# State-space layer: the products with the carried state of both channel halves stand together, ahead of the products within the chunks

## The chip, the cores and the metric

The kernel runs on one core of one Trainium2 chip. The metric is the device time of one execution in microseconds (us); less is better. Before the change it is 1345.12 us, the median of three runs (1344.85 to 1346.7).

## What is computed

The kernel is a trunk of two layers, in float32, for one sequence of 512 tokens and 1024 channels. The first layer mixes tokens with a short gated convolution, the second with a state-space mixer (Mamba-2, chunked form); a SwiGLU feed-forward network follows each. The change lies in the state-space mixer, which has 8 groups of 4 heads with 64 channels each. Cut to what matters, the reference is:

```python
def ssd_chunked(xh, dt, a, bm, cm):
    ...
    cb = jnp.einsum('bclgn,bcsgn->bclsg', cm, bm)
    y_diag = jnp.einsum('bclsgr,bcsgrp->bclgrp', cb[..., None] * decay, xdt)
    states = jnp.einsum('bclgn,bclgr,bclgrp->bcgrpn', bm, decay_to_end, xdt)
    ...
    _, prev = lax.scan(step, h0, (jnp.moveaxis(states, 1, 0), jnp.moveaxis(chunk_decay, 1, 0)))
    ...
    y_off = jnp.einsum('bclgn,bcgrpn,bclgr->bclgrp', cm, prev, jnp.exp(cs).astype(dtype))
    return (y_diag + y_off).reshape(bsz, s, g, r, p)
```

`y_off` is the part that the carried state `prev` gives; `y_diag` is the part from within a chunk. Both are added.

## The kernel before

The 512 tokens are cut into 4 chunks of 128 (`NCH = 4`). The 256 channels of a group are two halves `q` of 128, each with two heads of 64. The loop over the groups is a pipeline written out by hand: while group `g` goes through its state-space steps, the projections of group `g+1` (six of them, `ip`, each 24 matmuls of 128x128 by 512 at lines L276 to L278) fill the time of PE. A block `tc.manual_schedule` holds PE, ACT and DVE to the order in which the code issues their instructions; the listings below show what the build made of it.

The steps of a group are, in order: `step_a` (transposes `xtok` L1205 and `btokp` L1216, products `cb` L1222), `states` (products `st` L1238 and L1240, and on DVE the scan that makes `prev`, L1243 and L1245), `step_cc`, and `sums` (the squares of the result are summed over the channels by a product with ones, `ssg`, L1318, in the last group L1315). After `sums`, ACT takes the root (`rg`, L1322), DVE its reciprocal (L1326), and the result is scaled.

`step_cc` is what the change touches. For one half `q`, `step_c` issues on PE:

- 3 products `yo` (L1277), one for each chunk but the first: `prev` (128 x 128) is the stationary operand, so the whole array of 128 rows by 128 columns is used;
- 8 products `yd` (L1283), two heads in each of 4 chunks: a stationary operand of 128 x 64 each, with the output of one head on partitions 0 to 63 and of the other on 64 to 127, so each uses one half of the array's columns.

All of these are float32, and a float32 product shows as two records in the trace: 6 records of `yo`, 16 of `yd`. On DVE, `step_c` then issues four instructions: `y1` = `yo` times the decay (L1288), `y0` = `xs` times `d` plus `yd` (L1289), their sum (L1290), and the gate (L1291). ACT squares the result (L1294, L1297).

PSUM tiles of the tag `aux` (`xtok`, `btokp`, `cb`, `st`, `yo`, `yd`, `ssg`, and in the last group the tiles `y` of the second half of the output projection) go round in 4 buffers, in the order in which they are asked for. In the last group the PE work around `step_cc` is the output projection `y` (L378 to L380), whose weights `whlo` are copied by ACT (L203) and split by DVE (L204).

The weights of a projection come by DMA from SP's queue into `wst`, ACT copies the high part (L221) and DVE makes the low part (L222).

Of the kernel before, what the change touches and what calls it, by code (L numbers as in the profile page):

```python
# [35 lines left out]
def trunk_kernel(  # L36
# [23 lines left out]
    def aux_ps(name, shape=(P, T)):  # L60
        return ps.tile(list(shape), F32, tag="aux", name=name, bufs=4)

    def t2(name):
        return tmp.tile([P, T], F32, tag="t2", name=name, bufs=4)
# [505 lines left out]
    with ExitStack() as ph:  # L570
# [428 lines left out]
        with tc.manual_schedule(engines={PE_ENGINE, mybir.EngineType.SP, mybir.EngineType.Activation,  # L999
# [15 lines left out]
            for k in range(2 * NF - 6):  # L1015
# [8 lines left out]
                q, j = divmod(k - 3, 4)  # L1024
# [25 lines left out]
    with ExitStack() as ph:  # L1050
# [99 lines left out]
        class Group:  # L1150
# [114 lines left out]
                dve.tensor_tensor(e, e, flat(self.cbm).unsqueeze(1).to_broadcast([P, 2, T]), MUL)  # L1265

            def step_cc(self):
                self.step_c(0)
                self.step_c(1)

            def step_c(self, q):

                g = self.g
                pyo = aux_ps("yo")
                for cc in range(1, NCH):
                    sl = slice(cc * P, (cc + 1) * P)
                    pe.matmul(pyo[:, sl], self.prev[:, cc - 1, q * P:(q + 1) * P], self.ct[:, sl],  # L1277
                              start=True, stop=True)
                pyd = aux_ps("yd")
                for cc in range(NCH):  # L1280
                    sl = slice(cc * P, (cc + 1) * P)
                    for hh in range(2):
                        pe.matmul(pyd[hh * HD:(hh + 1) * HD, sl],  # L1283
                                  self.xdt[:, cc, (2 * q + hh) * HD:(2 * q + hh + 1) * HD],
                                  self.e[:, 2 * q + hh, sl], start=True, stop=True)
                y0 = yp.tile([P, T], F32, tag="y", name=f"yg{2 * g + q}")
                y1 = t2("y1")
                dve.tensor_mul(y1[:, P:], pyo[:, P:], self.ecs[:, q, P:])  # L1288
                dve.scalar_tensor_tensor(y0, self.xs[q], dcol[:, 2 * g + q:2 * g + q + 1], pyd, MUL, ADD)  # L1289
                dve.tensor_add(y0[:, P:], y0[:, P:], y1[:, P:])  # L1290
                dve.tensor_mul(y0, y0, self.zs[q])  # L1291
                if q == 0:
                    self.accg = t2("accg")
                    act.activation(self.accg, y0, AF.Square)  # L1294
                else:
                    sqg = t2("sqg")
                    act.activation(sqg, y0, AF.Square)  # L1297
                    if g < NG - 1:
                        pool.tensor_tensor(self.accg, self.accg, sqg, ADD)
                    else:  # L1300
                        dve.tensor_add(self.accg, self.accg, sqg)
                ygs.append(y0)
# [795 lines left out]
```

## Time and profile before

| | |
|---|---|
| time, median of 3 runs | 1345.12 us (1344.85 to 1346.7) |
| the profiled execution: its own time | 1345.17 us |
| the profiled execution: span from first to last instruction | 1343.0 us |
| granted TensorE clock, mean | 0.999 |
| PE busy | 1326.6 us (99%) |
| DVE busy | 985.2 us (73%) |
| ACT busy | 618.2 us (46%) |
| POOL busy | 65.3 us (5%) |

What lies outside the span is 1345.17 - 1343.0 = 2.17 us. In the rows of the trace, PE is the stream of matmuls and PEld that of the weight loads, which may run beside matmuls; DVE, ACT, POOL and SP are the other engines. A row of the timeline gives start, length, engine, line, operation and tiles, and how many records it merges; a bracket gives how long the engine was idle before it and what ended that. A row of the chain of waits gives start, length, and what the time went to. PE's record of a matmul is longer than the distance to the next one, since matmuls are pipelined, so the cost of a matmul on PE is read from the distance of two starts.

### The profile page before, as it was taken

The page shows a single profiled execution, that of the slowest core. Times are in us where ns is not written, and L with a number is a line of the kernel's source. Part 1 is how long each engine was busy: PE and PEld are TensorE (multiplying, and loading weights), DVE is VectorE, ACT ScalarE, POOL GpSimd, SP SyncE. Part 2 cuts the span into 40 slices and gives each one's busy share as a digit, 9 for nine tenths or more (in the row PEclk, how much of TensorE's full clock was granted, in tenths as well). Part 3 has the DMA queues.
Part 4 walks back from the last instruction along what each step waited for, and adds up shares of the span by engine and source line. Part 5 has one row for each costly group of instructions (what it writes and reads, how often), then busy time and mean ns, then how long its engine had stood idle before and what let it go on. Part 6 is the DMA issues. An engine that isn't in the chain of part 4 may idle for free.

```text
span 1343.0 us, 19136 instructions
## 1 busy us (share of the span) xinstructions
PE 1326.6 (99%) x7485; PEld 1143.8 (85%) x7485; DVE 985.2 (73%) x1581; ACT 618.2 (46%) x995; POOL 65.3 (5%) x82
## 2 busy tenths in 40 slices
PE   8999999999999999999999999999999999999997
PEld 7788889888888888898888888888889999998875
DVE  5588866778787322659889988888677777767887
ACT  5323356222323211665644555554474555544664
POOL 0000000000000000000000000000000111101320
PEclk9999999999999999999999999999999999999999
DMA  9757760777776322513543344423251788779851
GB/s 311 237 179 233 252 206 1 225 245 234 238 247 221 126 94 67 157 33 118 165 130 114 91 128 124 132 73 125 79 157 46 192 219 210 199 200 286 166 108 63
DMA packets 199886, 215.90 MB, mean 161 GB/s; under 512 B 8292, under 2 KB 148468, under 8 KB 198772
## 3 DMA queue, kind: packets, MB, share of 16 engines
q1 hardware_dynamic: 186384, 184.74, 44.3%
q0 software_dynamic: 9264, 17.04, 7.4%
q10 hardware_dynamic: 4148, 12.90, 3.0%
q8 instruction: 59, 0.97, 0.3%
q14 instruction: 31, 0.25, 0.1%
HBM read 195.37 MB, written 2.24 MB: 147 GB/s over the span
## 4 chain that ended last, share of the span: by engine, by line
PE 91%; issue 3%; DMA 2%; ACT 2%; DVE 1%; SPq 0%; DVEq 0%; ACTq 0%; POOLq 0%
PE ip L276 14%; PE ip L278 14%; PE ip L277 14%; PE sA L1694 6%; PE y L378 6%; PE y L380 6%; PE y L379 6%; PE cA L1789 4%; PE sC L1694 3%; PE li L756 2%; PE li L276 2%; PE li L277 2%; PE li L278 2%; PE sB L1694 2%; PE yd L1283 1%
## 5 line engine op out<-in xcount | busy, mean ns | idle before, releaser
L276 PE MATMUL ip<-h,whl 128*128 128x512 f32 x840 | 331.2, 394 | 0.2 <-DVE cv L863 0.2
L278 PE MATMUL ip<-h,whl 128*128 128x512 f32 x840 | 327.2, 390 | 0.0
L277 PE MATMUL ip<-h,whl 128*128 128x512 f32 x840 | 327.0, 389 | 0.0
L276 PEld LDWEIGHTS ip<-h,whl 128*128 128x128 f32 x840 | 157.8, 188 | 33.8 <-issue 1.8
L278 PEld LDWEIGHTS ip<-h,whl 128*128 128x128 f32 x840 | 157.7, 188 | 33.4
L277 PEld LDWEIGHTS ip<-h,whl 128*128 128x128 f32 x840 | 157.8, 188 | 31.6
L222 DVE TENSOR_TENSOR whl<-wst,whl 128x1024 fp32r<-128x1024 f32 x99 | 120.4, 1221 | 60.1 <-ACT whl L221 59.9
L124 DVE SCALAR_TENSOR_TENSOR ada_acc<-ada_st,csil,ada_acc 128x512 f32<-128x512 f32 x140 | 105.0, 750 | 3.9 <-DMA ada_st<-in_ada_w_dram 0.4
L204 DVE TENSOR_TENSOR whlo<-wsto,whlo 128x1024 fp32r<-128x1024 f32 x41 | 49.9, 1224 | 78.2 <-ACT whlo L203 78.0
L221 ACT CAST whl<-wst 128x1024 fp32r<-128x1024 f32 x99 | 103.0, 1041 | 3.2 <-DMA wst<-in_a_w_in_dram 1.8
L276 PE MATMUL li<-h,whl 128*128 128x256 f32 x288 | 83.2, 289 | 0.0
L278 PE MATMUL li<-h,whl 128*128 128x256 f32 x288 | 81.6, 283 | 0.0
L277 PE MATMUL li<-h,whl 128*128 128x256 f32 x288 | 81.5, 283 | 0.0
L203 ACT CAST whlo<-wsto 128x1024 fp32r<-128x1024 f32 x41 | 42.6, 1050 | 76.4 <-PE y L380 75.0
L1694 PE MATMUL sA<-tq,whl 128*128 128x256 f32 x576 | 74.6, 283 | 0.3 <-DVE g L1720 0.3
L1694 PEld LDWEIGHTS sA<-tq,whl 128*128 128x128 f32 x576 | 71.6, 192 | 0.6 <-DVE g L1720 0.5
L378 PE MATMUL y<-whlo,ff 128*128 128x512 f32 x176 | 68.6, 390 | 0.0
L380 PE MATMUL y<-whlo,ff 128*128 128x512 f32 x176 | 68.5, 389 | 0.0
L379 PE MATMUL y<-whlo,ff 128*128 128x512 f32 x176 | 68.5, 389 | 0.0
L1142 DVE SCALAR_TENSOR_TENSOR cu<-ip,cols,cu 128x511 f32<-128x511 f32 (+2 forms) x84 | 62.8, 747 | 3.9 <-ACT cu L1139 1.4
L1789 PE MATMUL cA<-whlo,ao 128*128 128x512 f32 x264 | 61.2, 390 | 4.4 <-ACT ao L1767 4.0
L1789 PEld LDWEIGHTS cA<-whlo,ao 128*128 128x128 f32 x264 | 49.3, 188 | 15.7 <-ACT ao L1767 4.8
(328 smaller groups left out, 2436.0 us busy)
## 6 DMA issues: line engine op xcount, KB each, us to landing
ada_st<-in_ada_w_dram SPq DMA_DIRECT2D x96, 512.0 KB, 5.2
wst<-in_f_w_in_dram SPq DMA_DIRECT2D x26, 1024.0 KB, 6.5
wst<-in_m_w_in_dram SPq DMA_DIRECT2D x14, 1024.0 KB, 5.4
wsto<-in_f_w_out_dram SPq DMA_DIRECT2D x10, 1024.0 KB, 5.1
wst<-in_m_w_in_dram SPq DMA_DIRECT2D x20, 512.0 KB, 5.2
wst<-in_a_w_in_dram SPq DMA_DIRECT2D x9, 1024.0 KB, 5.9
wsu<-in_f_w_in_dram SPq DMA_DIRECT2D x17, 512.0 KB, 5.8
csb<-cs_d ACTq DMA_DIRECT2D x8, 1024.0 KB, 5.2
```

The source lines that it names most:

```text
L124: dve.scalar_tensor_tensor(acc, w, csil[:, k:k + 1], acc, MUL, ADD)
L221: later.append((lambda sw=sw, w=w: act.copy(w[:, 0, :nk, :], sw), lambda sw=sw, w=w: dve.tensor_tensor(w[:, 1, :nk, :], sw, w[:, 0, :nk, : ...
L222: lambda sw=sw, w=w: dve.tensor_tensor(w[:, 1, :nk, :], sw, w[:, 0, :nk, :].bitcast(F32), SUB)))
L276: pe.matmul(dst, w_at(w, 0, kk), a[:, 0, sl], start=start, stop=False)
L277: pe.matmul(dst, w_at(w, 0, kk), a[:, 1, sl], start=False, stop=False)
L278: pe.matmul(dst, w_at(w, 1, kk), a[:, 0, sl], start=False, stop=stop)
L378: pe.matmul(pst, a[:, 0, tk], wt[:, 0, kk, :], start=k == 0, stop=False)
L379: pe.matmul(pst, a[:, 0, tk], wt[:, 1, kk, :], start=False, stop=False)
L380: pe.matmul(pst, a[:, 1, tk], wt[:, 0, kk, :], start=False, stop=k == K - 1)
L1142: dve.scalar_tensor_tensor(u[:, sft:], pst[:, :T - sft], w[3 - sft], u[:, sft:], MUL, ADD)
L1694: pe.matmul(dst, w[:, wl, k0 + k, :], moving(q, k, al), skip_group_check=True, start=q in ("P1", "P5", "P2") and k == 0 and i == 0, stop=k ...
L1789: pe.matmul(bank[r][sub], a[:, al, q, tk], w[:, hl, q, :], start=first and k == 0, stop=last and k == 2, skip_group_check=True)
```

## The change

`step_cc` now issues the `yo` products of both halves first and then calls `step_c` for each half, which gets its `yo` tile as an argument. Nothing else is edited; the lines behind move by 5.

```diff
             def step_cc(self):
-                self.step_c(0)
-                self.step_c(1)
-
-            def step_c(self, q):
-
-                g = self.g
+                off = [self.step_o(q) for q in range(2)]
+                for q in range(2):
+                    self.step_c(q, off[q])
+
+            def step_o(self, q):
+
                 pyo = aux_ps("yo")
                 for cc in range(1, NCH):
                     sl = slice(cc * P, (cc + 1) * P)
                     pe.matmul(pyo[:, sl], self.prev[:, cc - 1, q * P:(q + 1) * P], self.ct[:, sl],
                               start=True, stop=True)
+                return pyo
+
+            def step_c(self, q, pyo):
+
+                g = self.g
                 pyd = aux_ps("yd")
                 for cc in range(NCH):
                     sl = slice(cc * P, (cc + 1) * P)
```

PE's instructions in the second group, before (`ip` is the projection around the step; the names in brackets are the semaphores that an instruction waits for, by the engine or DMA queue that raises them):

```order
L278 MATMUL ip<-h_4402,whl 128x512
L1277 MATMUL yo<-ct,prev 128x128 [waits DVE_49,Activation_49]
L1277 MATMUL yo<-ct,prev 128x128 [waits DVE_49] x2
L1283 MATMUL yd<-csb,xdt 64x128 [waits DMAHW6_49,PE_49]
L1283 MATMUL yd<-csb,xdt 64x128 x7
L1277 MATMUL yo<-ct,prev 128x128 x3
L1283 MATMUL yd<-csb,xdt 64x128 x8
L276 MATMUL ip<-h_4395,whl 128x512
```

and in the changed kernel:

```order
L278 MATMUL ip<-h_4402,whl 128x512
L1277 MATMUL yo<-ct,prev 128x128 [waits DVE_49,Activation_49]
L1277 MATMUL yo<-ct,prev 128x128 [waits DVE_49] x2
L1277 MATMUL yo<-ct,prev 128x128 [waits PE_49]
L1277 MATMUL yo<-ct,prev 128x128 x2
L1288 MATMUL yd<-csb,xdt 64x128 [waits DMAHW6_49]
L1288 MATMUL yd<-csb,xdt 64x128 x15
L276 MATMUL ip<-h_4395,whl 128x512
```

The second half's three `yo` moved ahead of the first half's eight `yd`; the sixteen `yd` are one run. The wait of PE on its own count went with the buffer that `cb` had used: it was at the first `yd`, and is at the fourth `yo`. It asks for the same count in both kernels, that of the end of `cb`. The other seven groups read alike on PE.

DVE's instructions around `step_cc` in the last group, before (`ys` are operands of the output projection, `whlo` its weights, `y` and `yg` the tiles of L1288 to L1291):

```order
L1340 TENSOR_TENSOR ys<-yg_5710,ys 128x512 [waits Activation_49]
L1288 TENSOR_TENSOR y_7740<-yo,ecsb 128x384 [waits DMAHW1_49,DMAHW0_49,PE_49]
L1289 TENSOR_SCALAR yg_7739<-xs_6792,dcol,yd 128x512 [waits PE_49]
L204 TENSOR_TENSOR whlo<-wsto,whlo 128x1024 [waits DMAHW7_49,Activation_49]
L1290 TENSOR_TENSOR yg_7739<-yg_7739,y_7740 128x384 [waits DVE_49]
L1291 TENSOR_TENSOR yg_7739<-yg_7739,zs_7368 128x512 [waits DVE_49]
L1288 TENSOR_TENSOR y_7761<-yo,ecsb 128x384 [waits PE_49]
```

and in the changed kernel:

```order
L1345 TENSOR_TENSOR ys<-yg_5714,ys 128x512 [waits Activation_49]
L1293 TENSOR_TENSOR y_7744<-yo,ecsb 128x384 [waits DMAHW1_49,DMAHW0_49,PE_49]
L204 TENSOR_TENSOR whlo<-wsto,whlo 128x1024 [waits DMAHW7_49,Activation_49]
L1294 TENSOR_SCALAR yg_7743<-xs_6792,dcol,yd 128x512 [waits PE_49]
L1295 TENSOR_TENSOR yg_7743<-yg_7743,y_7744 128x384 [waits DVE_49]
L1296 TENSOR_TENSOR yg_7743<-yg_7743,zs_7368 128x512 [waits DVE_49]
L1293 TENSOR_TENSOR y_7761<-yo,ecsb 128x384
```

In the last group the split of `whlo` (L204) moved one place up, ahead of the instruction that reads the first `yd`. In the other seven groups DVE's instructions keep their order. The second half's L1293 has no wait for PE of its own any more, since the instruction ahead of it already waits for a later product. ACT's and POOL's instructions keep their order and their waits; one DMA on SP's queue (`gg`, L320) still waits for the first L1294 of the last group.

## The prediction, made before the changed kernel ran

> **What bounds the kernel now.** I read the page first, then the chain of waits through the eight groups (630 to 960 us), then the timeline of PE and DVE at the step, then the waits.
>
> ```profile
> span 1343.0 us, 19136 instructions
> PE 91%; issue 3%; DMA 2%; ACT 2%; DVE 1%; SPq 0%; DVEq 0%; ACTq 0%; POOLq 0%
> ```
>
> PE carries 91% of the chain that ended last. Inside the groups it carries all of it: the next view, the chain of waits, has no other engine between 633 and 943 us. Its rows give start, length and what the time went to; here are the second group's step, the small products of the third group that stand between, and the third group's step.
>
> ```profile
> 681.01 0.67 PE yo L1277 x6
> 681.68 1.02 PE yd L1283 x16
> 682.71 0.86 PE yo L1277 x6
> 683.57 1.02 PE yd L1283 x16
> 684.60 0.43 PE ip L276
> ...
> 707.04 0.87 PE xtok L1205 x8
> 707.91 0.33 PE btokp L1216 x3
> 708.24 0.89 PE cb L1222 x8
> ...
> 721.37 0.67 PE yo L1277 x6
> ```
>
> The first `yo` of a group to that of the next is 721.37 - 681.01 = 40.36 us. Busy time by stretch, for exactly one such period (columns: length, then busy time of PE, PEld, DVE, ACT, POOL):
>
> ```profile
> 842.27:882.62 40.35, 40.35 (x216) 33.78 (x215) 35.62 (x58) 21.22 (x27) 1.30 (x1) 1.00 0.39 118
> ```
>
> PE is busy for 40.35 of 40.35 us at full granted clock (1.00); DVE has 4.7 us to spare. So in this stage a matmul that costs PE less shortens the period by as much, until DVE's spare time is gone.
>
> **The change, part by part.** No product is added or taken away: 6 `yo` and 16 `yd` per group and the same operands. What changes is how often PE goes from the full array (`yo`, 128 x 128) to half the columns (`yd`, 128 x 64) and back. Before: in, out, in, out. After: in, out. The chain above has the price of each.
>
> *The plain pitch.* The first `yo` row is 0.67 us for 6 records, 0.11 each, so going from `ip` to `yo` costs nothing. `xtok`, `btokp` and `cb` (0.87 for 8, 0.33 for 3, 0.89 for 8) have the same 0.11 across three changes of tile and PSUM buffer: a new tile as such is free. For `yd` I take a stretch inside a run, and the length of one record:
>
> ```profile
> 722.24 0.82 PE L1283 MATMUL yd<-csb,xdt 128*64 128x128 f32 x12
> L1283 PE MATMUL yd<-csb,xdt x256: 272/273/324, 641.3 to 937.3; 128*64 128x128 f32 x128
> ```
>
> Twelve records are six pairs, since the two column halves run side by side; (0.82 - 0.27) / 5 = 0.11 us a pair.
>
> *Going in* (`yo` to `yd`): the `yd` row is 1.02 where 8 pairs at 0.11 are 0.88, so about 0.15. *Going out* (`yd` to anything): the second `yo` row is 0.86, not 0.67, so 0.19; the `ip` row behind the last `yd` is 0.43, and the chain's plain pitch of such a matmul is 0.23 (the row of L379 below), so 0.20. The waits agree that nobody is waited for when it goes out:
>
> ```profile
> PEld yo L1277 <- issue: 1.4, 8, 0.2
> PEld ip L276 <- issue: 1.2, 7, 0.2
> DVE rg L1326 <- ACT rg L1322: 15.8, 6, 3.3
> DVE yg L1289 <- PE yd L1283: 2.4, 5, 0.5
> ```
>
> Eight times (once a group) the weight load of the second `yo` sat 0.17 us with no releaser. [...]
>
> So each group saves one way in and one way out, 0.15 + 0.19 = **0.34 us**. Lower bound for a group 0.15 (only one of the two goes), upper bound 0.40 (both at 0.20). *The moved wait:* the fourth `yo` now waits for PE's own count at the end of `cb`, 13 us earlier (708.24 against 721.37). The first three `yo` also carry waits, long met, and keep the 0.11 pitch, so I cost it at nothing; bounds 0 and 0.17 (the idle above).
>
> *DVE in groups 3 to 7.* The first `yo` ends as before, but the first `yd` now comes after six more `yo` records and ends 0.11 x 6 = 0.66 us later; less 0 to 0.05 for its own pairs, 0.62 to 0.66. Where DVE is early it waits longer, with its whole queue behind it: L1290, L1291, the second half, then the convolution (L1142) and the weight splits (L222). The sixth group, before:
>
> ```profile
> 843.13 0.56 DVE L1288 TENSOR_TENSOR y<-yo,ecsb 128x384 f32<-128x384 f32 x1 [0.56 <-PE yo L1277]
> 844.17 0.75 DVE L1289 SCALAR_TENSOR_TENSOR yg<-xs,dcol,yd 128x512 f32<-128x512 f32 x1 [0.48 <-PE yd L1283]
> 853.09 0.68 DVE L1309 TENSOR_TENSOR sqs<-accg,sqs 128x512 fp32r<-128x512 f32 x1
> 856.95 0.61 PE L1318 MATMUL ssg<-sqs,ones_r 128*128 128x512 f32 x2
> ```
>
> Who waits for it: the nearest is `ssg`, whose operand is ready at 853.77 and which PE reaches at 856.95, 3.2 us later. DVE 0.66 late and PE 0.34 early leave 2.2. The lateness does not add up from group to group: L1326 above idles 15.8 / 6 = 2.6 us each time for ACT, which PE's `ssg` sets. So it is hidden, and the price if that cover went is in the rivals. The row above counts five waits of L1289 for `yd`, one in each of these groups; in the first two DVE arrives later, and the delay is smaller or none.
>
> *The last group* has no such cover, since `ssg` follows after 9 us and is waited for. Its rows (timeline, then the chain):
>
> ```profile
> 933.85 0.83 PE L1277 MATMUL yo<-ct,prev 128*128 128x128 f32 x6
> 934.58 1.04 ACT L203 CAST whlo<-wsto 128x1024 fp32r<-128x1024 f32 x1
> 934.61 1.09 PE L1283 MATMUL yd<-csb,xdt 128*64 128x128 f32 x16
> 935.31 0.55 DVE L1288 TENSOR_TENSOR y<-yo,ecsb 128x384 f32<-128x384 f32 x1
> 935.78 0.74 DVE L1289 SCALAR_TENSOR_TENSOR yg<-xs,dcol,yd 128x512 f32<-128x512 f32 x1
> 936.43 1.22 DVE L204 TENSOR_TENSOR whlo<-wsto,whlo 128x1024 fp32r<-128x1024 f32 x1
> 937.57 0.55 DVE L1290 TENSOR_TENSOR yg<-yg,y 128x384 f32<-128x384 f32 x1
> 941.99 0.69 DVE L1301 TENSOR_TENSOR accg<-accg,sqg 128x512 f32<-128x512 f32 x1 [0.70 <-ACT sqg L1297]
> 942.88 0.41 PEld L1315 LDWEIGHTS ssg<-accg,ones 128*128 128x128 f32 x2
> 945.81 0.40 PE L380 MATMUL y<-whlo,ys 128*128 128x512 f32 x1
> ...
> 942.81 0.23 PE y L379
> 943.35 1.05 ACT whlo L203
> 945.71 0.70 ACT rg L1322
> 946.45 0.50 PE y L378
> ```
>
> The first `yd` ends at 935.70 now and at about 936.36 then. DVE's order has the split L204 ahead of its reader: L204 starts at 935.78 (its ACT copy ended at 935.62) and takes 1.14 to the next start, so the reader starts at 936.92 and waits for nothing, and L1290 follows 0.78 later (the distance of these two in the sixth group, 844.17 to 844.95, is the same), at 937.70: 0.13 late, not 0.66. `accg` is ready at 942.81; PE arrives at `ssg` 0.34 earlier, at 942.54, and stands about 0.3 us. That is free, because three tiles later PE waits anyway: it could start the fourth `y` at 945.81 + 0.23 = 946.04 but starts at 946.45, when ACT's `rg` frees the buffer. ACT's chain begins when the `y` product ahead of `ssg` ends, all of it 0.34 earlier, so the fourth `y` starts at 946.11. The group gains its 0.34 (0 if DVE were the 0.66 late). SP's `gg` DMA, released by that reader, moves from 936.54 to about 937.7; the next on that queue goes at 945.69, so nothing waits for it.
>
> Sum: 8 x 0.34 = 2.7 us, span 1340.3, time of the profiled execution 1345.17 - 2.7 = 1342.5; it lies 0.05 above the median, so against the median **1342.4 us**.
>
> **Rivals.**
>
> *Half the gain.* The second `yo` may still pay for itself, if what costs in it is the first load of other weights, or the moved wait holds it 0.17. For it: the price of the way out shows in the second `yo`, not in the last `yd`. Against it: `xtok` to `btokp` to `cb` loads other weights at 0.11. Then 0.15 to 0.19 a group, 1.2 to 1.5 in all: 1343.6 to 1343.9.
>
> *The gain is taken back further on.* After the groups the chain leaves PE:
>
> ```profile
> 1003.60 33.00 issue
> 1037.13 4.92 DMA wsu<-wsu
> ...
> PE sA L1694 <- DVE g L1720: 0.3, 1, 0.3
> SPq L1636 <- DVE tq L1822: 35.8, 1, 35.8
> ```
>
> PE meets this chain at 1056 us and already waits 0.3 for it. If it did not move, PE would wait 2.7 more and the time would stay at 1345.1. Against it: its DMAs are released by DVE (`tq`, after 35.8 us of waiting), which follows PE.
>
> *Slower: DVE sets the pace.* DVE takes its queue in order, so the late `yd` holds up what PE needs next. If DVE's spare time were gone, the five groups in which L1289 now waits (the row: 5 times) would each last 0.62 longer and the gain would be lost too: 5 x 0.62 = 3.1, 1348.2. It decides once DVE is later than the 3.2 us ahead of `ssg` less the 0.34; the 2.6 us idle at L1326 and the 4.7 us spare in a period speak against it. [...]
>
> **How the numbers follow.** The forecast has 0.70; half the gain 0.12; taken back 0.08; slower 0.10. A measurement of this kernel tells a difference from none at about 0.2%, here 2.69 us or 1342.43. The forecast lies on that line: with 0.34 to 0.36 a group (the rows are rounded to 0.01) it is 2.7 to 2.9, so I put 0.55 of its 0.70 beyond the line and 0.15 within. Faster 0.55, within 0.35, slower 0.10. The forecast's own range, 0.28 to 0.40 a group, is 1341.9 to 1342.9; taking in half the gain and leaving out most of the other two gives 1341.8 to 1344.2.
>
> **What would show it.** In the changed trace: one `yo` row of 12 at about 1.33 us in the chain and one `yd` row of 32 at about 1.9; PEld idle without releaser once a group, not twice; a period of 40.0 us, not 40.36; L1294 waiting about 1.1 us for `yd` in groups 3 to 7 and L1331 less than 2.6 for ACT; `ssg` of the last group waiting about 0.3 and the fourth `y` following ACT's `rg` as before. I am wrong if the second `yo` keeps a first distance of 0.2, if PE waits for DVE at any `ssg` of the first seven groups, or if PE's wait at 1056 grows by what the groups gained.

## The result and the profile after

| | before | after |
|---|---|---|
| time, median (range), runs | 1345.87 us (1344.85 to 1348.22), 9 | 1342.96 us (1342.35 to 1344.11), 9 |
| the profiled execution: time, span | 1345.17, 1343.0 us | 1344.11, 1341.9 us |
| granted clock of that execution | 0.999 | 0.997 |

The ratio is 0.9977, with a 95% interval of 0.9967 to 0.9987: the change makes the kernel 2.9 us faster, 0.2%. 1342.4 had been predicted.

The head of the page of the changed kernel, and the line by engine of the chain that ended last:

```profile
span 1341.9 us, 19122 instructions
PE 93%; DVE 2%; SPq 2%; ACT 1%; DMA 1%; issue 1%; DVEq 0%; ACTq 0%
```

The chain is still PE's. Its rows of the changed kernel (start, length, what the time went to), at the places that were shown of before: the second group's step and the third group's first `yo`:

```profile
680.97 1.34 PE yo L1277 x12
682.31 1.90 PE yd L1288 x32
684.21 0.43 PE ip L276
...
720.99 1.34 PE yo L1277 x12
```

Twelve `yo` records take 1.34, twice the 0.67 of six: the second three no longer pay for a way out. The 32 `yd` take 1.90, which is 16 pairs at 0.11 plus one way in. The group still pays one way out, in the `ip` row of 0.43. From the first `yo` to the second matmul behind the step, the distance was 4.007 us in the eight groups (within 0.002) and is 3.662 (within 0.001): 0.345 less. First `yo` to first `yo` is now 720.99 - 680.97 = 40.02. Busy time in one period of the changed kernel (length, then PE, PEld, DVE, ACT, POOL, granted clock, and last the DMAs' share and GB/s):

```profile
840.87:880.88 40.01, 40.01 (x216) 33.73 (x215) 35.60 (x58) 21.22 (x27) 1.30 (x1) 1.00 0.38 119
```

PE is as full as it was, 40.01 of 40.01, and DVE's spare time is 4.4 instead of 4.7. The waits of the changed kernel in the groups (total us, times, longest):

```profile
DVE rg L1331 <- ACT rg L1327: 10.3, 6, 2.2
DVE yg L1294 <- PE yd L1288: 5.7, 5, 1.1
PEld ip L276 <- issue: 1.2, 7, 0.2
PEld ssg L1320 <- PE y L380: 0.4, 1, 0.4
```

DVE stands for `yd` five times as before, but 1.1 us each instead of 0.5, and its wait for ACT's `rg` has shrunk from 15.8 to 10.3. The row of PEld without a releaser at `yo` (8 times) is gone; the one at `ip` stayed. The last row is the last group's `ssg`. Its surroundings in the timeline of the changed kernel (a bracket is the idle time before):

```profile
931.81 1.50 PE L1277 MATMUL yo<-ct,prev 128*128 128x128 f32 x12
933.73 1.22 DVE L204 TENSOR_TENSOR whlo<-wsto,whlo 128x1024 fp32r<-128x1024 f32 x1
934.86 0.74 DVE L1294 SCALAR_TENSOR_TENSOR yg<-xs,dcol,yd 128x512 f32<-128x512 f32 x1
935.63 0.34 SPq L320 DMA_DIRECT2D gg<-gate_d  x1
935.64 0.56 DVE L1295 TENSOR_TENSOR yg<-yg,y 128x384 f32<-128x384 f32 x1
940.06 0.69 DVE L1306 TENSOR_TENSOR accg<-accg,sqg 128x512 f32<-128x512 f32 x1 [0.70 <-ACT sqg L1302]
940.87 0.30 PEld L1320 LDWEIGHTS ssg<-accg,ones 128*128 128x128 f32 x2 [0.42 <-PE y L380]
943.32 0.69 ACT L1327 ACTIVATE rg<-ssg,eps 128x512 f32<-128x512 f32 x1
944.06 0.50 PE L378 MATMUL y<-whlo,ys 128*128 128x512 f32 x1
```

All starts here are read against the first `yo` of the group, since the whole stage lies 2.0 us earlier (931.81 against 933.85). L204 goes first and L1294 follows at 3.05, where it was at 1.93; L1295 starts at 3.83 where it was at 3.72, 0.11 late. `accg` is served 0.11 late (8.25 against 8.14), PE stands about 0.3 at `ssg` (its two records stand 0.42 and 0.50 behind the record ahead of them, where the plain pitch is 0.23 and before had 0.43 for the second), and the fourth `y` comes 0.05 behind the end of ACT's `rg` (944.01), as the 946.45 followed 946.41 before. Measured from the first `yo` of the first group, that `y` came 305.96 us later before and comes 303.26 later now: 2.70 less.

Behind the groups PE meets the feed-forward network's chain as before: `sA` waits 0.3 us for DVE in both kernels (the waits of the changed kernel, then PE's row behind that wait in the chain):

```profile
PE sA L1699 <- DVE g L1725: 0.3, 1, 0.3
1053.46 3.14 PE sA L1699 x24
```

`sA` started at 1056.18 before, so DVE's chain came along with PE.

### Where another 0.3 us came from, and where 1.6 went

The groups give 2.70 of the profiled difference, yet the span is only 1.1 shorter. Two things lie behind the groups, and neither was in the prediction.

First, a small gain. Between the groups and the feed-forward network PE makes transposes `xtr` (L494) of what ACT normalizes (L485). The chain of before, and the wait it stands for:

```profile
991.24 1.24 ACT xn L485 x2
992.52 0.55 PE xtr L494 x3
PEld xtr L494 <- ACT xn L485: 0.5, 1, 0.5
```

In the changed kernel there is no such wait; the same chain there never leaves PE (`989.92 0.44 PE xtr L494 x4`). The stretch from the first `xtr` to the first `li` behind it is 2.5 us where PE waits and 2.2 where it doesn't. Measured from the first `yo`, the first `li` is 3.02 us earlier than before.

Second, a loss in this execution. Near the end PE waits twice for 2.0 us for ACT's `ao`, in both kernels. Here is the profiled execution of the changed kernel around the first pause in three pieces of 3.41 us (length, busy time of PE, PEld, DVE, ACT, POOL, then the granted clock and the DMAs):

```profile
1297.36:1300.77 3.41, 1.39 (x7) 0.86 (x5) 3.41 (x7) 3.21 (x6) 0.00 (x0) 1.00 0.02 3
1300.77:1304.18 3.41, 3.41 (x8) 2.65 (x9) 2.78 (x5) 0.00 (x0) 0.00 (x0) 0.50 0.00 0
1304.18:1307.59 3.41, 3.41 (x16) 2.81 (x15) 1.62 (x3) 2.28 (x5) 0.00 (x0) 1.00 0.00 0
```

In the piece after the pause the granted clock is 0.50 for exactly 3.41 us, and PE makes 8 matmuls where it makes 16 in the next one. The profiled execution of before had no such stretch there: its granted clock is 1.00 throughout from 1298 to 1312. Measured from the first `li` in both, PE's stream is 1.61 us behind that of before when the stretch is over, and 1.68 at its last product. So the spans close: -3.02, +1.68, and a stream that began 0.31 later (the first `yo` of all at 640.80 against 640.49) make -1.03, and 1341.9 - 1343.0 is -1.1.

The times of both kernels lie in two heaps some 1.5 us apart. Of 25 further runs of the kernel before, 16 lie at 1344.84 to 1345.87, all with a mean granted clock of 0.999, and 9 at 1346.46 to 1347.49, all with 0.998 or 0.997. A stretch of 3.41 us at 0.50 takes 1.7 us, 0.0013 of the span. So a stretch of half clock is the likely difference in before too, though its one profile shows none ahead of the end. The nine runs in the table part less cleanly: 1342.96, 1343.0 and 1343.43 of the changed kernel lie between the heaps. Heap against heap, the change is worth 2.8 us (medians of the lower heaps 1345.2 and, in the repeated measurement below on the same chip, 1342.4) and 2.9 (1346.8 and 1343.9).

### The profile page after: what moved, and what is told of

It is laid out like the page before. It is cut to its first block, busy times and chain, and to the rows that moved or that the text cites. A ratio compares the mean times of both kernels' runs of the same rounds, so it can differ in the third digit from the quotient of the medians.

```text
span 1341.9 us, 19122 instructions
## 1 busy us (share of the span) xinstructions
PE 1326.1 (99%) x7485; PEld 1144.7 (85%) x7485; DVE 985.1 (73%) x1581; ACT 617.9 (46%) x995; POOL 65.2 (5%) x82
## 4 chain that ended last, share of the span: by engine, by line
PE 93%; DVE 2%; SPq 2%; ACT 1%; DMA 1%; issue 1%; DVEq 0%; ACTq 0%
PE ip L276 14%; PE ip L278 14%; PE ip L277 14%; PE sA L1699 6%; PE y L378 6%; PE y L379 6%; PE y L380 6%; PE cA L1794 4%; PE sC L1699 3%; PE li L276 2%; PE li L278 2%; PE li L277 2%; PE sB L1699 2%; PE li L756 1%; PE yd L1288 1%; PE cD L1794 1%
## 5 line engine op out<-in xcount | busy, mean ns | idle before, releaser
L204 DVE TENSOR_TENSOR whlo<-wsto,whlo 128x1024 fp32r<-128x1024 f32 x41 | 49.9, 1223 | 78.0 <-ACT whlo L203 77.9
```

## The experiments

Two theories stand against each other. *Switches*: PE pays for each change from the full array to half the columns and back, 0.15 and 0.19 to 0.20, and all else is hidden. *Place*: what counts is that `yo` of the second half lies ahead of `yd`, by its wait, its buffers or what DVE gets when. A third question is how much cover DVE's lateness has.

### The same number of switches, another order

`yo` of the first half, `yd` of both, `yo` of the second half: two switches as in the change, but the second `yo` stays behind. (Left out here: `step_d`, the `yd` loop taken out of `step_c` unchanged.)

```diff
-                off = [self.step_o(q) for q in range(2)]
-                for q in range(2):
-                    self.step_c(q, off[q])
+                o0 = self.step_o(0)
+                d0, d1 = self.step_d(0), self.step_d(1)
+                o1 = self.step_o(1)
+                self.step_c(0, o0, d0)
+                self.step_c(1, o1, d1)
```

> In every group the order on PE is now: yo of the first half, yd of both halves, yo of the second half. The two yo are not together, but PE goes in and out of the half-column shape once a group, as in the change. Theory (the price is the number of switches of shape, 0.35 us for one way in and one way out): the step lasts as long as in the change, and the kernel is 2.7 to 2.8 us faster than before, as the change is; the wait of DVE for the first yd does not grow (0.5 us in the groups where it waits, against 1.1 in the change). Rival (what pays is that the second yo has its own weights loaded behind another yo): the gain is 1.5 us or less.

Measured: 1343.77 us (1342.0 to 1345.38, 11 runs), ratio to before 0.998 (0.9972 to 0.9989). Its chain in the third group, and DVE's wait for `yd`:

```profile
721.10 0.67 PE yo L1279 x6
721.77 1.90 PE yd L1289 x32
723.67 0.86 PE yo L1279 x6
DVE yg L1300 <- PE yd L1289: 2.2, 5, 0.5
```

The way out is now paid by the second `yo` (0.86) and no longer by `ip`, and the step is 3.662 us, the change's to the nanosecond; the fourth `y` of the last group stands at 303.15 from the first `yo`, against 303.26. DVE waits 0.5 for `yd`, as before, and not 1.1. Two things follow: the gain is the two switches, and DVE's longer wait in the change costs at most the 0.11 by which this order is ahead at that `y`; at the first `li` the two are 0.02 apart. By the medians the gain is only 2.1 us and not the 2.7 to 2.8 expected, as 7 of the 11 runs lie at 1343.69 and above, all with a granted clock of 0.998 or less; the other four are 1342.0 to 1342.42 with 0.999. Against the heaps of the 22 runs of before on this chip (medians 1345.1 and 1347.0) the gain is 2.7 and 3.0.

### The change in every other group

```diff
+                if self.g % 2:
+                    for q in range(2):
+                        self.step_c(q, self.step_o(q))
+                    return
                 off = [self.step_o(q) for q in range(2)]
```

> The change in four of the eight groups only (the first, third, fifth, seventh); the others keep the order of before. Theory: each changed group is 0.35 us shorter and the others are as before, so periods of 40.0 and 40.36 us and 1.4 us less than before in all. Rival (the gain comes from elsewhere, as from the last group or from the phase of DMAs): periods do not follow the order of the group, and the gain is 0 or the full 2.7.

Measured: 1345.38 us (1344.11 to 1346.27, 10 runs), ratio 0.9995 (0.9986 to 1.0005). By the median this is no change, where 1.4 us had been expected. Its chain at the `yo` of the third, the fourth and the fifth group:

```profile
721.26 1.34 PE yo L1281 x12
...
761.27 0.67 PE yo L1281 x6
...
762.96 0.86 PE yo L1281 x6
...
801.62 1.34 PE yo L1281 x12
```

The groups alternate, 40.01 us and 40.35, and the fourth `y` of the last group lies 1.35 earlier than before, half of 2.70. So each group pays for itself, without help from its neighbours. The median taken alone would have pointed to the rival's gain of 0: eight of the ten runs have a granted clock of 0.998 or less. Heap against heap on this chip, the two runs with 0.999 are 0.8 faster than before and the other eight 1.6, which brackets the 1.4 without fixing it.

### Seven switches each way in a group

For each chunk `yo` and then its `yd`: seven ways in and seven out instead of one each (`yo` and `yd` of a half are made in one loop over `cc`; only that loop is shown).

```diff
+                for cc in range(NCH):
+                    sl = slice(cc * P, (cc + 1) * P)
+                    if cc:
+                        pe.matmul(pyo[:, sl], self.prev[:, cc - 1, q * P:(q + 1) * P], self.ct[:, sl],
+                                  start=True, stop=True)
+                    for hh in range(2):
+                        pe.matmul(pyd[hh * HD:(hh + 1) * HD, sl],
+                                  self.xdt[:, cc, (2 * q + hh) * HD:(2 * q + hh + 1) * HD],
+                                  self.e[:, 2 * q + hh, sl], start=True, stop=True)
```

> In every group yo and yd alternate chunk by chunk, so PE goes in and out of the half-column shape 7 times a group where it was 2 times before. Theory: 5 more pairs at 0.35 us in each of 8 groups, 13.8 us slower than before. Rival (a switch is dear only behind a long run, or in and out overlap when they follow closely): less than 7 us slower.

Measured: 1359.57 us (1358.89 to 1360.63, 4 runs), ratio 1.01 (1.0086 to 1.0113): 13.7 us slower than before. Its chain inside the fourth group:

```profile
767.81 0.42 PE yo L1277 x2
768.23 0.37 PE yd L1280 x4
...
769.81 0.59 PE yd L1280 x8
```

Two `yo` records at 0.11 are 0.22, and the row has 0.42: 0.20 for the way out, every time. Two pairs of `yd` are 0.22, and the row has 0.37: 0.15 for the way in; the row of four pairs, 0.44, has 0.59. The step is 5.648 us, 1.986 more than with one switch each way, which is 0.331 for each of six further pairs of switches. This is the clearest measurement of the price, as it is taken six times over.

### No switch at all

From the order of before, each pair of `yd` is one product over all 128 columns that takes the decay of the first of the two heads.

```diff
-                    for hh in range(2):
-                        pe.matmul(pyd[hh * HD:(hh + 1) * HD, sl],
-                                  self.xdt[:, cc, (2 * q + hh) * HD:(2 * q + hh + 1) * HD],
-                                  self.e[:, 2 * q + hh, sl], start=True, stop=True)
+                    pe.matmul(pyd[:, sl], self.xdt[:, cc, q * P:(q + 1) * P], self.e[:, 2 * q, sl],
+                              start=True, stop=True)
```

> The order of before, but each pair of yd products of 64 columns is one product of 128 columns that uses the decay of the first head for both, so the second head of each half gets the wrong decay: this leaves out half of the streams. Four products of two records at 0.11 are 0.88 us, as eight pairs were, so PE streams as long, with no switch of shape at all. Theory (the shape pays): all four switches of a group go, 0.69 us a group, 5.3 to 5.6 us faster than before. Rival (the change of tile, of weights or of PSUM buffer pays): no faster than before by more than 0.5 us.

Measured: 1341.91 us (1341.19 to 1343.11, 5 runs), ratio 0.9969 (0.9957 to 0.9981). Its chain in the third group:

```profile
721.60 0.67 PE yo L1277 x6
722.27 0.89 PE yd L1282 x8
723.16 0.67 PE yo L1277 x6
723.83 0.89 PE yd L1282 x8
724.73 0.23 PE ip L276
```

The order is that of before, and each surcharge is gone: the second `yo` is 0.67, `yd` 0.89, `ip` 0.23. The step is 3.355 us, 0.652 less than before, and the fourth `y` of the last group lies 5.24 earlier, 8 x 0.655, just short of the 5.3 to 5.6 expected: 16 full-width records of `yd` at 0.112 take 0.04 more than 16 pairs at 0.109. This rules out the place of `yo`, the first load of other weights and the wait as causes: all three are as before. Besides the shape, only the number of `yd` records differs, 16 in place of 32; but the surcharge isn't one by the record, since behind the first two pairs the pairs of before stand at the plain 0.11. End to end only 3.9 us arrive, as all five runs carry a granted clock of 0.998, that of the upper heap; against the upper heap of the runs of before on this chip (1347.0) it is 5.1.

### DVE made late

The first half's L1293 is issued seven times instead of once in the first seven groups, with the change's order on PE.

```diff
                 dve.tensor_mul(y1[:, P:], pyo[:, P:], self.ecs[:, q, P:])
+                if q == 0 and g < NG - 1:
+                    for _ in range(6):
+                        dve.tensor_mul(y1[:, P:], pyo[:, P:], self.ecs[:, q, P:])
```

> The change, with the first DVE instruction of the step (yo times the decay, 0.55 us) issued seven times instead of once in the first seven groups; its result is the same. DVE is then 2.8 to 3.6 us later at the operand of ssg. Theory (DVE's lateness is hidden up to the distance at ssg, 2.2 us in the change, 0.9 in the first group): PE waits 0.6 to 1.4 us for ssg in each of the groups 2 to 6, 1.9 to 2.7 in the first, and the kernel is 5 to 12 us slower than the change. Rival (there is more cover than that, or DVE was on the path already): no slower than the change by more than 1 us, or 7 x 2.8 = 20 us slower.

Measured: 1353.65 us (1353.07 and 1354.23), ratio 1.0058 (1.004 to 1.0076). That is 10.5 us slower than the change beside it (1343.13), inside the 5 to 12 expected, but by luck, as the cost is not spread as expected: only the first group's wait is of the size that was said. The periods are 44.21, 40.59, 40.14, 40.12, 40.11, 40.12 and 54.73 us, where the change has 40.01 or 40.02 for the first six and 50.93 for the last. DVE in the sixth group, first in the changed kernel and then here:

```profile
841.73 0.56 DVE L1293 TENSOR_TENSOR y<-yo,ecsb 128x384 f32<-128x384 f32 x1 [0.57 <-PE yo L1277]
843.44 0.75 DVE L1294 SCALAR_TENSOR_TENSOR yg<-xs,dcol,yd 128x512 f32<-128x512 f32 x1 [1.15 <-PE yd L1288]
852.36 0.68 DVE L1314 TENSOR_TENSOR sqs<-accg,sqs 128x512 fp32r<-128x512 f32 x1
```

```profile
846.84 0.56 DVE L1293 TENSOR_TENSOR y<-yo,ecsb 128x384 f32<-128x384 f32 x1 [0.46 <-PE yo L1277]
847.44 3.52 DVE L1296 TENSOR_TENSOR y<-yo,ecsb 128x384 f32<-128x384 f32 x6
850.87 0.74 DVE L1297 SCALAR_TENSOR_TENSOR yg<-xs,dcol,yd 128x512 f32<-128x512 f32 x1
859.78 0.69 DVE L1317 TENSOR_TENSOR sqs<-accg,sqs 128x512 fp32r<-128x512 f32 x1
```

The six copies take 3.43 us (847.44 to 850.87), but they run into the time in which DVE stood for `yd` anyway, so `sqs` comes only 2.31 later: 12.94 behind L1293 instead of 10.63. The change leaves 2.17 us between the end of `sqs` and `ssg` in the second to the sixth group, where before left 3.18. 2.31 less 2.17 is 0.14, and the period grew by 0.11. So the cover of 2.2 that the prediction worked out is right to a tenth. The expectation forgot the 1.15 that the copies fill.

What costs here is elsewhere. In the first group DVE is late and stands for nothing: PE waits 0.91 and 1.10 at `ssg`, and the granted clock is 0.50 from 658.74 to 662.15. Ahead of the last group PE waits 0.84 and 0.80 for `ys`. The mean granted clock of this execution is 0.995 where that of before has 0.999; at 1.7 us for each of 1350.9, that is, as an estimate, about three such stretches. The two long periods together, with what the half clock adds to them, are 8.0 us longer than the change's; the second group, with 0.6, still has a rest of the first one's delay (PE waits 0.24 at `ssg`). In the first group the change has a cover of 0.94 and not of 2.2 (before had 1.61), and of its own lateness in these two places PE sees nothing.

### The last group left out

The order of before in the last group alone, that of the change in the other seven.

```diff
+                if self.g == NG - 1:
+                    for q in range(2):
+                        self.step_c(q, self.step_o(q))
+                    return
```

> The change in the first seven groups; the last group has the order of before on PE and on DVE. Theory: the last group gave 0.3 us of the gain, so PE's fourth output tile behind ssg is 7 x 0.345 = 2.4 us earlier than before, not 2.7. Rival (the last group gave nothing, as its ssg waits for DVE): the tile is as early as in the change.

Measured: 1343.69 us (1342.73 to 1344.77, 8 runs), ratio 0.9983 (0.9973 to 0.9993). The fourth `y` of the last group stands at 303.62 us from the first `yo`, 0.36 behind the change's 303.26. The last group gives its 0.34, although PE stands at `ssg` there.

### The change again

> The changed kernel once more, beside the next one on the same chip. Theory: the times fall into two heaps, about 1342.4 and 1343.9 us; the later ones are executions in which the granted clock is halved for 3.4 us in one of the two pauses of 2 us that PE makes near the end.

Measured: 1343.13 us (1342.17 to 1344.17, 10 runs), ratio 0.9981 (0.9972 to 0.999). Five runs are at 1342.17 to 1342.62 and five at 1343.65 to 1344.17, and none is between. The profiled execution, with a span of 1340.2 us, had a mean granted clock of 0.999 and 1.00 around the first pause; its landmarks agree with the first profile's within 0.01 us up to `li` (351.14 against 351.13 from the first `yo`), and the last product of PE comes 1.65 us earlier.

### The pauses filled

The change, with 16 small products that nobody reads put into PE's stream at the two pauses.

```diff
+                if n in (28, 34):
+                    for _ in range(16):
+                        pe.matmul(bank["C"][0][:, :P], ones_r, ones_r, start=True, stop=True, skip_group_check=True)
```

> The changed kernel with 16 products of 128 columns, whose result nobody reads, in each of the two pauses of 2 us near the end. Theory (the halved clock follows PE's pause): the upper heap disappears, all executions lie within 0.7 us of 1342.4, median 0.3 to 1 us below that of the changed kernel beside it. Rival (the drop has another cause): two heaps as before, or the products hold up the real ones and the time rises by 0.5 us or more.

Measured: 1342.4 us (1342.15 to 1343.27, 10 runs), ratio 0.9977 (0.9968 to 0.9986). PE at the first pause:

```profile
1298.40 1.90 PE L2053 MATMUL cC<-ones_r 128*128 128x128 f32 x16
1300.59 3.66 PE L1794 MATMUL cA<-whlo,ao 128*128 128x512 f32 x15 [0.29 <-ACT ao L1772]
```

The pause is 0.29 instead of 2.02, the `cA` behind it start when they would have anyway, and all ten runs lie below 1343.3: the upper heap is gone. (One run, 1343.27, lies 0.9 above 1342.4, where all had been expected within 0.7.) Beside the change's 1343.13 on the same chip the median is 0.7 us lower. By its median it is the fastest version that computes the whole output.

## Why the prediction was right, point by point

- *PE sets the period, so what PE saves shortens it.* Right: 40.36 to 40.01 or 40.02, with PE busy throughout.
- *0.15 in, 0.19 to 0.20 out, 0.34 for a group.* Right: the step is 0.345 shorter in each of the eight groups. The two `yd` of a pair do run side by side: in the third group of before they start 0.007 apart, and the next pair 0.109 behind (722.235, 722.241, 722.344). With no switch it lost 0.652, with six more pairs it gained 1.986. "Half the gain" falls with it: the second `yo` has no first distance of its own left, and in the kernel without switches the first load of other weights and the old wait cost nothing.
- *The moved wait costs nothing.* Right: the twelve `yo` are at the plain pitch.
- *DVE is 0.62 to 0.66 later, and hidden.* Right in groups 3 to 7: L1294 starts 2.57 behind the first `yo` instead of 1.90 and waits 1.1 instead of 0.5, L1295 follows it in order (844.22 behind 843.44 in the sixth group, 0.78 as before), L1331 idles less (10.3 instead of 15.8), 2.17 us are left ahead of `ssg`, and the run with a late DVE puts the edge of the cover within 0.1 of that. This is why "DVE sets the pace" did not happen. Not right is that the delay is "smaller or none" in the first two groups: DVE hardly stands for `yd` there, PE gains on it, and `sqs` ends 0.32 and then 0.68 later behind the first `yo`; the first group's cover of 0.94 is the smallest of the seven, and it was enough.
- *The last group keeps its 0.34.* Right, step by step: L204 first, L1295 0.11 late (0.13 said), PE stands at `ssg`, the fourth `y` follows ACT's `rg`; 0.36 by the run that leaves this group out. `gg` went at 935.63, 3.82 behind the first `yo`, where 937.7 was 3.85 behind it, and nothing waited.
- *The gain is not taken back at 1056.* Right: that chain came 2.72 us earlier, and the wait is 0.3 in both.
- *Sum 2.7.* Right for the groups (2.70 at the fourth `y`, 8 x 0.345 = 2.76; the long last period shrank by 0.307 only). The whole is 2.8 to 2.9 heap against heap. At the first `li` it is 3.02, of which 0.3 comes from the lost wait at `xtr`; this term was missing. Why ACT is in time there is not settled: the kernels without a wait and those with one (before, the one with seven switches, the one with none) don't fall in the order of their lateness, and it was not tried.
- *1342.4.* The measured median, 1342.96, lies just outside the forecast's own 1341.9 to 1342.9. The base had moved as well: nine runs of before have a median of 1345.87, three had 1345.12. How near the two medians come to 2.7 is in part luck, since each depends on how many of nine runs fell into the upper heap; the landmarks within the traces don't.
- *What the prediction did not see* is what moves a single run by more than half the gain: the half clock behind a pause (1.61 us of PE's stream in the changed kernel's first profile). The page of before showed 4.0 us of PE's waiting for ACT's `ao`, and its times already ran from 1344.85 to 1346.7.

## What to carry to other kernels

Put products that use the whole array together, and those that use a part of its columns together: here each way in and out cost 0.35 us, as much as one and a half float32 products of 128 columns (two records of 0.11 each), while changing tile, weights or buffer cost nothing (the records stayed 0.11 apart; without switches six `yo` behind `yd` took 0.67). Before a reordering on the bounding engine is taken for free, follow the engine behind it to the next point at which it is waited for, and take its standing time off the delay before comparing it with the slack. When the effect is a fifth of a per cent, compare landmarks within the traces (here from the first product of the stage to a product behind it: 351.13, 351.14 and 351.15 us to the first `li` in three profiles of this order) and look at the clock near PE's pauses before believing a difference of medians.

## What the runs showed of the hardware

The half clock came in whole steps of 3.413 us. In the clock records of the two profiles of before and after, the stretches ahead of the half clock at the end are 1334.611 us of full clock before, and 1293.651 full, 3.413 half and 34.133 full after: 391, 379, 1 and 10 times 3.4133. With the late DVE, half clock lasted 3.41 us from 658.74. What goes with it is how much of a pause falls into one step. In the changed kernel's first profile, the step that ends at 1300.77 holds the whole pause of 2.02 us, and the next has half clock; with the late DVE, PE idles 1.99 of the 3.41 us ahead of 658.74. In the repeated run of the change the same pause was cut, as the clock of its pieces shows:

```profile
1295.94:1299.35 3.41, 2.68 (x12) 1.88 (x10) 3.41 (x6) 2.26 (x5) 0.00 (x0) 1.00 0.10 17
1299.35:1302.76 3.41, 2.12 (x9) 1.80 (x10) 3.41 (x6) 1.17 (x3) 0.00 (x0) 1.00 0.00 0
```

PE idles 0.73 and 1.29 us in the two pieces, and the clock stays at 1.00, in the 3.41 us behind them too. The steps of the other pauses of about 2 us, counted from the changes of the clock, have 1.75 us of idle PE (1299.72 to 1303.13) and 1.57 (1316.78 to 1320.19) in before and 1.68 (1317.83 to 1321.24) in the changed kernel, each with a clock of 1.00 in the step behind it. The amount alone may not decide it: with the late DVE, the two waits of 0.84 and 0.80 us ahead of the last group seem to have had half clock behind them too, as that period is 3.80 us longer than the change's (54.73 against 50.93), more than the waits make up (an estimate). So which heap an execution falls into seems to depend on how the steps cut a pause. That is read from these four traces and not shown by an experiment: no run moved the steps or a pause against them. That the pauses matter is shown by the run that fills them.

The second thing is the asymmetry: going into the column halves takes 0.15 us (1.02 for eight pairs of 0.11) and leaving them 0.19 to 0.20, the same whether `yo` (0.86 for 0.67), `ip` or `y` (0.43 for 0.23 each) stands behind, and in all the orders tried.
